# Feed-forward inputs with the activations held in TensorE and the weights passing, and a way through DRAM that turns the results

## The chip, the cores and the metric

The kernel runs on one core of one Trainium2 chip. The metric is the device time of one execution in microseconds (us), taken as the median of several runs. Of the core's engines, TensorE (PE) multiplies, VectorE (DVE), ScalarE (ACT) and GpSimd (POOL) do the work element by element, and SyncE (SP) issues most of the transfers.

## The reference

A small decoder trunk: 256 positions of width 1024, two layers, float32. Each layer is a feed-forward half step, a mixer (a gated short convolution in the first layer, sparse attention in the second), and another feed-forward half step. So there are four feed-forwards, which this change is about:

```
def rmsnorm(x, g):
    xf = x.astype(jnp.float32)
    y = xf * lax.rsqrt(jnp.mean(xf * xf, axis=-1, keepdims=True) + EPS)
    return (y * g.astype(jnp.float32)).astype(x.dtype)

def swiglu_ffn(x, w_in, w_out):          # w_in: 1024 x 5632, w_out: 2816 x 1024
    gate, up = jnp.split(x @ w_in, 2, axis=-1)
    return (jax.nn.silu(gate) * up) @ w_out

for i in range(DEPTH):
    ...
    h = h + 0.5 * swiglu_ffn(rmsnorm(h, ffn1_norm[i]), ffn1_w_in[i], ffn1_w_out[i])
    hn = rmsnorm(h, mix_norm[i])
    h = h + (short_conv_mixer(hn, ...) if i < N_A_LAYERS else nsa_mixer(hn, ..., kv))
    h = h + 0.5 * swiglu_ffn(rmsnorm(h, ffn2_norm[i]), ffn2_w_in[i], ffn2_w_out[i])
```

## The kernel before

The residual h lies in SBUF turned, with features on partitions: 8 tiles of 128 features x 256 positions. Every number that goes into a product is split in two (hi and lo, both in TensorE's fp32r form), and three of the four partial products are made: hi x hi, lo x hi, hi x lo. A tile of activations, xs[k], is 128 x 512: 256 positions of hi, then 256 of lo.

Weights come as one long stream (class Stream). A load brings 128 x 2048 numbers (1 MB) into one of three ws buffers; ScalarE casts half of such a load to hi (high, tile wh), VectorE subtracts to get lo (low, tile wl). Such a half is a unit of 128 x 1024; up to six units are held. take hands units to the products, done gives them back, and pump splits as many further ones as there is room for. Where pump, high and low are called in the program sets the order in which ScalarE and VectorE do this work between their other work. All engines run their own instructions in the order of the program and wait for each other by semaphores.

A feed-forward's input (ffn_in) makes 22 hidden tiles of 128 features. For each tile f it holds the weights in TensorE and lets the activations pass: for gate and for up, 8 wide matmuls (wh[k] held, xs[k] with all 512 columns passing, which gives hi x hi and lo x hi side by side) and 8 narrow ones (wl[k] held, the 256 hi columns passing). From the fifth tile on, two tiles are interleaved (lines 425 and 430). The result is in PSUM with hidden features on partitions: total adds the two halves (L367, L368), times multiplies by the norm's factor per position (R, 128 x 256; L372), ffn_evac applies Silu and multiplies (L384, L385), and split makes the hi and lo of the hidden tile hid[f] (L361, L362). The factor R comes from Norm.rows: a matmul of all ones with the sums of squares gives it on all partitions.

The projection out (out_proj) holds a tile of w_out and lets hid[f] pass, 22 wide and 22 narrow matmuls for each of 8 output tiles (L498, L504), mostly two output tiles interleaved. out_evac adds the result to h and makes the next stage's xs.

The first feed-forward is different at its start: first_tiles makes three hidden tiles while the inputs still arrive (L574), and their sums wait for the norm's factor.

The K/V projection (b_full, L762 to L764) and the queries' projection already hold activations: per k and per half of the positions (tt), hi is held and wh passes (512 columns), lo is held and wh passes, hi is held and wl passes. The result has positions on partitions.

Of the kernel before, what the change touches and what calls it, by code (L numbers as in the profile page):

```python
# [12 lines left out]
AF = mybir.ActivationFunctionType  # L13
# [3 lines left out]
P = 128  # L17
# [24 lines left out]
THIRD = {1: (0, 2), 3: (2, 4), 6: (4, 8)}  # L42
LINE, FIXED = 256, 160
HOMES = (("ones", [P, P], F32), ("V0", [P, 512], F32), ("V1", [P, 512], F32), ("vc", [P, 2, 2, 64], F32R),
         ("cs0", [P, 8, 4, 16], F32R), ("cs1", [P, 8, 4, 16], F32R), ("cbias", [P, 8, 2, 2, 16], F32),
# [23 lines left out]
def trunk(ctx, tc, A, out):  # L69
# [29 lines left out]
    def bank2():  # L99
        return mk([P, 2, 512], "mm", 2, pool=ps)  # L100
# [300 lines left out]

    def ffn_in(xs, norm, R=None, bg=None, pre=None, sums=()):

        hid, sums = [], list(sums)
        box = [R]
        n0 = len(sums)

        def mid():
            if pre is not None:
                pre()  # L410
            box[0] = norm.rows()

        def finish(f, o):
            sums.append(total(o, 2))
            late = len(sums) > 1
            weave(ffn_evac(sums.pop(0), box[0], hid), not late or f == n0 + 5)
            if late and f - n0 in (3, 7, 9):
                list(ffn_evac(sums.pop(0), box[0], hid))
            if bg is not None:
                bg(f)  # L420

        def wide(o, us, ks, last=8):
            for x in range(2):
                for k in ks:
                    pe.matmul(o[:, x], us[x][0][:, k * P:(k + 1) * P], xs[k], start=(k == 0), stop=(k == last))  # L425

        def narrow(o, us, last=8):
            for x in range(2):
                for k in range(8):
                    pe.matmul(o[:, x, :T], us[x][1][:, k * P:(k + 1) * P], xs[k][:, :T], start=False, stop=(k == last))  # L430

        f = n0
        while f < NF:
            o = bank2()
            if f < n0 + 4 or f + 1 == NF:
                a_group([o[:, 0], o[:, 1]], xs, mid if f == n0 and R is None else None, not n0)
                finish(f, o)
                f += 1
                continue

            u = W.take(2)
            wide(o, u, range(8))
            o2, u2 = bank2(), W.take(2)
            wide(o2, u2, [0])
            narrow(o, u, 7)
            W.done(2, False)
            finish(f, o)
            narrow(o2, u2)
            wide(o2, u2, range(1, 8), 7)
            W.done(2, False)  # L450
            finish(f + 1, o2)
            f += 2
        return hid

# [17 lines left out]

    def out_proj(lhs, factor, norm, final=False):

        n, i, u = len(lhs), 0, None
        head = []
        if n == 8:
# [29 lines left out]

        c = len(head)
        while c < ND - final:
            o, run = bank(), []  # L510
            if n > 8 and c % 2 and c + 1 < ND - final:
                wide(o, run, range(n))
                o2, run2 = bank(), []
                wide(o2, run2, [0])
                narrow(o, run, range(n), n - 1)
                out_evac(o, c, factor, norm)
                narrow(o2, run2, range(n), free=False)
                wide(o2, run2, range(1, n), n - 1)
                for _ in range(sum(t[2] for t in run2)):
                    W.done(1, False)  # L520
                out_evac(o2, c + 1, factor, norm)
                W.pump()
                c += 2
                continue
            for ks in (range(n - 1), [n - 1]) if c == 0 else (range(n),):
                wide(o, run, ks)
                narrow(o, run, ks, n - 1)
            out_evac(o, c, factor, norm, n == 8)
            c += 1
# [135 lines left out]

    sums, parts_sq = first_tiles()
    hid = ffn_in(xs, First(), sums=sums)
    xs = new_xs()
    nm = Norm([(xs, G_MIX)])
    out_proj(hid, 0.5, nm)  # L670
    nm.halves()
# [67 lines left out]

    hid = ffn_in(xs, nm, pre=lambda: list(tab), bg=bias_bg)  # L740

# [4 lines left out]
    nm = Norm([(xkv, G_KV), (xs, G_FFN1 + 8)])  # L746
    out_proj(hid, 0.5, nm)
    nm.halves()
# [61 lines left out]
    def kv_cols(k):  # L810
# [4 lines left out]
        for tt in range(2):  # L815
            pe.transpose(pt[:, tt * P:(tt + 1) * P], kv["R"][:, tt * P:(tt + 1) * P], ident)
        kv["rc"] = sm([P, 2])
        ve.tensor_copy(out=kv["rc"], in_=pt[:, 0:2 * P:P])
# [165 lines left out]

    hid = ffn_in(xs, None, R1, bg)
    xs = new_xs()
    nm = Norm([(xs, G_MIX + 8)])
    out_proj(hid, 0.5, nm)
    del hid
# [333 lines left out]
    del oT  # L1323
    hid = ffn_in(xs, nm)

# [3 lines left out]

    out_proj(hid, 0.5, Store(), True)  # L1330

# [8 lines left out]
def _layout(i):  # L1340
# [3 lines left out]
    for n in ("ffn1", "ffn2"):  # L1344
        w = a[n + "_w_in"]
        r[n + "_w_in"] = w.reshape(2, 8, 128, 2, NF, 128).transpose(0, 2, 4, 3, 1, 5).reshape(2, 128, -1)
        r[n + "_w_out"] = np.stack([_rows(w) for w in a[n + "_w_out"]])

# [62 lines left out]
```

## Time and profile before

| | |
|---|---|
| median of 3 runs | 964.38 us (964.18 to 964.45) |
| the profiled execution | 964.34 us, span 962.6 us |
| TensorE matmuls | busy 958.2 us (100% of the span), 5618 recorded |
| VectorE, ScalarE, GpSimd | busy 725.5, 580.7, 128.8 us |
| traffic | 178.14 MB, 185 GB/s in the mean |
| TensorE's granted clock | 0.999 |

A matmul's duration in the trace runs from its issue to its modelled end and overlaps the next one's, so the distance from start to start says what one costs. Rows of a timeline give the start, the time, the engine, the line, and how many instructions were merged; rows of groups give the busy time, the mean duration of one in ns, and the idle time before them with what ended it.

### The profile page before, as it was taken

The page shows a single profiled execution, that of the slowest core. Times are in us where ns is not written, and L with a number is a line of the kernel's source. Part 1 is how long each engine was busy: PE and PEld are TensorE (multiplying, and loading weights), DVE is VectorE, ACT ScalarE, POOL GpSimd, SP SyncE. Part 2 cuts the span into 40 slices and gives each one's busy share as a digit, 9 for nine tenths or more (in the row PEclk, how much of TensorE's full clock was granted, in tenths as well). Part 3 has the DMA queues.
Part 4 walks back from the last instruction along what each step waited for, and adds up shares of the span by engine and source line. Part 5 has one row for each costly group of instructions (what it writes and reads, how often), then busy time and mean ns, then how long its engine had stood idle before and what let it go on. Part 6 is the DMA issues. An engine that isn't in the chain of part 4 may idle for free.

```text
span 962.6 us, 14572 instructions
## 1 busy us (share of the span) xinstructions
PE 958.2 (100%) x5618; PEld 841.9 (87%) x5618; DVE 725.5 (75%) x1154; ACT 580.7 (60%) x984; POOL 128.8 (13%) x212
## 2 busy tenths in 40 slices
PE   9999999999999999999999999999999999999998
PEld 8888888888888888888888888889877888888888
DVE  7898875678898787765758789767589798778643
ACT  7666653555466665644648876745489776566430
POOL 2000001154420000000121012000147110000000
PEclk9999999999999999999999999999999999999999
DMA  8565544545546874545536566445511256455541
GB/s 308 219 219 189 205 175 175 209 176 195 188 173 221 233 236 176 196 158 215 219 132 203 189 216 246 175 175 210 193 44 46 92 211 224 175 192 202 180 158 57
DMA packets 28898, 178.14 MB, mean 185 GB/s; under 512 B 3179, under 2 KB 6763, under 8 KB 8220
## 3 DMA queue, kind: packets, MB, share of 16 engines
q1 hardware_dynamic: 28684, 176.95, 51.1%
q8 instruction: 44, 0.72, 0.3%
q10 hardware_dynamic: 144, 0.26, 0.1%
q14 instruction: 26, 0.21, 0.1%
HBM read 175.59 MB, written 1.08 MB: 184 GB/s over the span
## 4 chain that ended last, share of the span: by engine, by line
PE 99%; ACT 0%; DVE 0%; issue 0%
PE mm L425 26%; PE a L498 17%; PE mm L430 14%; PE mm L353 10%; PE a L504 9%; PE mm L358 5%; PE a L353 4%; PE a L358 2%; PE mm L1127 1%; PE mm L574 1%; PE a L1204 1%; PE a L762 1%; PE a L764 1%; PE a L763 1%; PE a L1172 1%; PE a L574 1%
## 5 line engine op out<-in xcount | busy, mean ns | idle before, releaser
L182 DVE TENSOR_TENSOR wl<-ws,wh 128x1024 fp32r<-128x1024 f32 x318 | 392.5, 1251 | 48.1 <-ACT wh L165 30.9
L165 ACT CAST wh<-ws 128x1024 fp32r<-128x1024 f32 x318 | 327.0, 1045 | 35.8 <-PE a L498 12.3
L425 PE MATMUL mm<-xs,wh 128*128 128x512 f32 x1088 | 254.9, 390 | 0.0
L425 PEld LDWEIGHTS mm<-xs,wh 128*128 128x128 f32 x1088 | 201.6, 188 | 40.1
L498 PE MATMUL a<-act,wh 128*128 128x512 f32 x714 | 167.0, 390 | 0.0
L498 PEld LDWEIGHTS a<-act,wh 128*128 128x128 f32 x714 | 132.7, 188 | 26.8
L430 PEld LDWEIGHTS mm<-xs,wl 128*128 128x128 f32 x1088 | 135.3, 192 | 2.6
L430 PE MATMUL mm<-xs,wl 128*128 128x256 f32 x1088 | 136.8, 283 | 0.0
L368 DVE TENSOR_TENSOR t<-mm,t 128x512 f32<-128x512 f32 x95 | 65.4, 688 | 72.9 <-ACT t L367 72.2
L367 ACT COPY t<-mm 128x512 f32<-128x512 f32 x95 | 55.6, 586 | 94.2 <-PE mm L430 47.0
L353 PE MATMUL mm<-xs,wh 128*128 128x512 f32 x400 | 96.8, 392 | 0.0
L504 PEld LDWEIGHTS a<-act,wl 128*128 128x128 f32 x714 | 89.0, 192 | 1.8
L504 PE MATMUL a<-act,wl 128*128 128x256 f32 x714 | 89.9, 283 | 0.0
L353 PEld LDWEIGHTS mm<-xs,wh 128*128 128x128 f32 x400 | 73.3, 188 | 13.9
L314 POOL TENSOR_TENSOR sq<-sq,t 128x256 f32<-128x256 f32 x35 | 27.7, 791 | 389.1 <-ACT t L312 389.0
L457 DVE SCALAR_TENSOR_TENSOR base<-a,base 128x256 f32<-128x256 f32 x78 | 32.8, 422 | 57.0 <-PE a L498 54.7
L297 ACT ACTIVATE xs<-base 128x256 fp32r<-128x256 f32 x48 | 24.0, 504 | 79.0 <-DVE base L457 69.7
L384 ACT ACTIVATE t<-t 128x256 f32<-128x256 f32 x88 | 36.8, 418 | 52.7 <-DVE t L372 52.7
L372 DVE TENSOR_TENSOR t<-t,R 128x512 f32<-128x512 f32 x88 | 61.5, 699 | 2.6
L361 ACT CAST act<-t 128x256 fp32r<-128x256 f32 x96 | 39.0, 407 | 29.8 <-DVE t L691 19.4
L358 PEld LDWEIGHTS mm<-xs,wl 128*128 128x128 f32 x400 | 52.1, 191 | 2.4
L358 PE MATMUL mm<-xs,wl 128*128 128x256 f32 x400 | 52.8, 283 | 0.0
(274 smaller groups left out, 910.7 us busy)
## 6 DMA issues: line engine op xcount, KB each, us to landing
ws<-in_ffn_w_in_dram SPq DMA_DIRECT2D x85, 1024.0 KB, 4.7
ws<-in_ffn_w_out_dram SPq DMA_DIRECT2D x44, 1024.0 KB, 4.6
ws<-in_conv_w_in_dram SPq DMA_DIRECT2D x12, 1024.0 KB, 4.6
ws<-in_w_kv_dram SPq DMA_DIRECT2D x6, 1024.0 KB, 5.3
ws<-in_conv_w_out_dram SPq DMA_DIRECT2D x4, 1024.0 KB, 4.8
ws<-in_attn_w_q_dram SPq DMA_DIRECT2D x4, 1024.0 KB, 4.9
ws<-in_attn_w_o_dram SPq DMA_DIRECT2D x4, 1024.0 KB, 4.9
base<-row_d SPq DMA_DIRECT2D x8, 256.0 KB, 6.1
```

The lines of the kernel that those rows point to most:

```text
L165: ac.copy(h, src)
L182: ve.tensor_tensor(out=l, in0=src, in1=h.bitcast(F32), op=ALU.subtract)
L353: pe.matmul(o, u[0][:, k * P:(k + 1) * P], xs[k], start=(k == 0), stop=False)
L358: pe.matmul(o[:, :T], u[1][:, k * P:(k + 1) * P], xs[k][:, :T], start=False, stop=(k == last))
L361: ac.copy(dst[:, :T], src)
L367: ac.copy(r, o[:, :, T:])
L368: ve.tensor_tensor(out=r, in0=o[:, :, :T], in1=r, op=ALU.add)
L372: ve.tensor_tensor(out=r, in0=r, in1=R[:, None, :].to_broadcast([P, n, T]), op=ALU.mult)
L425: pe.matmul(o[:, x], us[x][0][:, k * P:(k + 1) * P], xs[k], start=(k == 0), stop=(k == last))
L430: pe.matmul(o[:, x, :T], us[x][1][:, k * P:(k + 1) * P], xs[k][:, :T], start=False, stop=(k == last))
L498: pe.matmul(o, run[k][0], lhs[k], start=(k == 0), stop=(k == last))
L504: pe.matmul(o[:, :T], run[k][1], lhs[k][:, :T], start=False, stop=(k == last))
```

## The change

All four feed-forward inputs are now made like the K/V projection (ffn_tokens). A pair g of hidden tiles (256 hidden features) is one pass: the weights are laid out so that 512 columns hold 256 gate and 256 up features, and per k and per half of the positions three matmuls of 512 columns are made. The first feed-forward keeps the old form for its first four tiles (a shortened ffn_in) and does so from pair 2 on.

The result has positions on partitions and features along the row, and out_proj needs it the other way round. So per pair: ScalarE applies Silu to the gate half straight from PSUM, with the norm's factor as its scale per partition; VectorE multiplies by the up half and by the factor, and turns blocks of 32 x 32 in place (turned). The tile of 128 x 2 x 256 is written to DRAM (sent), and read back in another order of its blocks, 32 numbers at a time (placed). That leaves features on partitions in an order of its own, which the rows of w_out follow (a new layout on the host). Then the tile is split into hi and lo as before (halved). These steps are spread over the next pairs: pair g is turned and sent at k = 1 of pair g + 1, read back at k = 7 of it (k = 5 if it is the last pair, then on ScalarE's queue instead of SP's), and split at k = 5 of pair g + 2. The last pair is sent and read back on ScalarE's queue after the loop, and split by rest(), which out_proj calls after the first 20 of 22 hidden tiles of its first two output tiles. The factor per position comes from Norm.cols, per partition, and is taken at the last k of a stage's first pair; the third feed-forward uses the factors of the K/V stage (rc).

```diff
+FROM = {"ffn1": (2, 0), "ffn2": (0, 0)}
...
+    def ffn_in(xs, norm, sums):
+
+        hid, sums, box = [], list(sums), []
+        us = W.take(2)
+        o = bank2()
+        a_pass([(o[:, x], us[x], xs, range(8)) for x in range(2)], mid=lambda: box.append(norm.rows()))
+        W.done(2, False)
+        sums.append(total(o, 2))
+        for r in sums:
+            weave(ffn_evac(r, box[0], hid))
+        return hid
+
+    def ffn_tokens(xs, norm=None, rc=None, bg=None, pre=None, hid=()):
+
+        hid, box = list(hid), [rc]
+        n0, last = len(hid) // 2, NF // 2 - 1
...
+        def turned(o):
+            rc, tb = box[0], t2([P, 2, T])
+            for tt in range(2):
+                s = t1()
+                ac.activation(s, o[:, tt, :T], AF.Silu, scale=rc[:, tt:tt + 1])
+                ve.scalar_tensor_tensor(out=s, in0=o[:, tt, T:], scalar=rc[:, tt:tt + 1], in1=s, op0=ALU.mult, op1=ALU.mult)
+                ve.transpose(tb[:, tt], s)
+            return tb
+
+        def sent(tb, eng):
+            d = mk([2, P, T], "turn", 3, pool=dr)
+            eng.dma_start(d.rearrange("t p n -> p t n"), tb)
+            return d
+
+        def placed(d, eng):
+            ht = t2([P, 2, T])
+            eng.dma_start(ht.rearrange("p f (c j) -> p f c j", j=32), d.rearrange("t (a i) (c f j) -> (i c) f (t a) j", i=32, f=2, j=32))
+            return ht
...
+        for g in range(n0, last + 1):
+            o = bank2()
+            for k in range(8):
+                if k % 2 == 0:
+                    u, = W.take()
+                if k == 7 and box[0] is None:
+                    mid()
+                wh, wl = [u[x][:, (k % 2) * 512:(k % 2 + 1) * 512] for x in range(2)]
+                for tt in range(2):
+                    sh, sl = xs[k][:, tt * P:(tt + 1) * P], xs[k][:, T + tt * P:T + (tt + 1) * P]
+                    pe.matmul(o[:, tt], sh, wh, start=(k == 0), stop=False)
+                    pe.matmul(o[:, tt], sl, wh, start=False, stop=False)
+                    pe.matmul(o[:, tt], sh, wl, start=False, stop=(k == 7))
+                if k % 2 == 0:
+                    continue
+                if k == 1 and old is not None:
+                    way = sent(turned(old), sy)
+                if k == 5 and ready is not None:
+                    halved(ready)
+                    ready = None
+                if k == (5 if g == last else 7) and way is not None:
+                    ready, way = placed(way, ac if g == last else sy), None
+                W.done(1, g < last or k < 7)
+            old = o
...
+        tb = turned(old)
+        halved(ready)
+        ready = placed(sent(tb, ac), ac)
+        W.pump()
+        return hid, lambda: halved(ready)
...
+        if rest is not None:
+            runs = [(bank(), []) for _ in range(2)]
+            for x, (o, run) in enumerate(runs):
+                run += [tile() for _ in range(n)]
+                wide(o, run, range(n - 2))
+                narrow(o, run, range(n - 2), n - 1, not x)
+            rest()
+            for x, (o, run) in enumerate(runs):
+                wide(o, run, range(n - 2, n))
+                narrow(o, run, range(n - 2, n), n - 1, False)
...
-    hid = ffn_in(xs, First(), sums=sums)
+    hid = ffn_in(xs, First(), sums)
+    hid, rest = ffn_tokens(xs, nm, hid=hid)
...
-    out_proj(hid, 0.5, nm)
+    out_proj(hid, 0.5, nm, rest=rest)
```

How it moves instructions. On TensorE, in the middle of a feed-forward, before: a tile's held weights change with every matmul and the activations pass (mm is the PSUM tile, and the operand behind the arrow is the passing one first).

```order
L425 MATMUL mm_566<-xs_121,wh_497 128x512
L425 MATMUL mm_566<-xs_122,wh_497 128x512
L425 MATMUL mm_583<-xs_115,wh_543 128x512
L425 MATMUL mm_583<-xs_115,wh_550 128x512
L430 MATMUL mm_566<-xs_115,wl_492 128x256
L430 MATMUL mm_566<-xs_116,wl_492 128x256
```

The same place after:

```order
L461 MATMUL mm_1029<-wh_981,xs_122 128x512
L462 MATMUL mm_1029<-wh_981,xs_122 128x512
L463 MATMUL mm_1029<-wl_985,xs_122 128x512
L461 MATMUL mm_1117<-wh_1005,xs_115 128x512
L462 MATMUL mm_1117<-wh_1005,xs_115 128x512
L463 MATMUL mm_1117<-wl_1007,xs_115 128x512
```

All matmuls are 512 wide now, and one pair follows the other without interleaving.

On VectorE, at the start of the first feed-forward, before (wl are weights' lo parts, act hidden tiles, the t tiles their way from PSUM):

```order
L362 TENSOR_TENSOR act_397<-t_58_388,act_397 128x256
L368 TENSOR_TENSOR t_64_433<-mm_400,t_64_433 128x512
L372 TENSOR_TENSOR t_39_295<-t_39_295,R_362 128x512
L182 TENSOR_TENSOR wl_439<-ws_336,wh_437 128x1024
L385 TENSOR_TENSOR t_67_441<-t_67_441,t_39_295 128x256
L182 TENSOR_TENSOR wl_448<-ws_336,wh_444 128x1024
L362 TENSOR_TENSOR act_450<-t_67_441,act_450 128x256
L368 TENSOR_TENSOR t_73_486<-mm_453,t_73_486 128x512
L372 TENSOR_TENSOR t_41_316<-t_41_316,R_362 128x512
L182 TENSOR_TENSOR wl_492<-ws_393,wh_490 128x1024
```

And after:

```order
L363 TENSOR_TENSOR act_397<-t_58_388,act_397 128x256
L183 TENSOR_TENSOR wl_402<-ws_336,wh_400 128x1024
L183 TENSOR_TENSOR wl_408<-ws_336,wh_404 128x1024
L373 TENSOR_TENSOR t_39_295<-t_39_295,R_362 128x512
L386 TENSOR_TENSOR t_68_411<-t_68_411,t_39_295 128x256
L363 TENSOR_TENSOR act_414<-t_68_411,act_414 128x256
L373 TENSOR_TENSOR t_41_316<-t_41_316,R_362 128x512
L386 TENSOR_TENSOR t_70_418<-t_70_418,t_41_316 128x256
L363 TENSOR_TENSOR act_421<-t_70_418,act_421 128x256
L373 TENSOR_TENSOR t_55_380<-t_55_380,R_362 128x512
L386 TENSOR_TENSOR t_72_425<-t_72_425,t_55_380 128x256
L363 TENSOR_TENSOR act_428<-t_72_425,act_428 128x256
```

The three waiting hidden tiles are finished one after the other with no weights between them; before, one tile's steps alternated with weights.

On ScalarE, at the end of the first feed-forward, before (the last two tiles leave PSUM between casts of weights):

```order
L367 COPY t_219_1312<-mm_1243 128x512
L165 CAST wh_1316<-ws_1219 128x1024
L384 ACTIVATE t_222_1320<-t_219_1312 128x256
L165 CAST wh_1323<-ws_1219 128x1024
L361 CAST act_1329<-t_222_1320 128x256
```

After, from the read of the next-to-last pair to the split of the last (turn is the tile in DRAM):

```order
L441 DMA t_224_1181<-turn_1139 128x16x32
L166 CAST wh_1183<-ws_1113 128x1024
L429 ACTIVATE t_228_1200<-mm_1117,rc_493 128x256
L429 ACTIVATE t_229_1204<-mm_1117,rc_493 128x256
L362 CAST act_1208<-t_224_1181 128x256
L362 CAST act_1211<-t_224_1181 128x256
L436 DMA turn_1214<-t_227_1199 128x2x256
L441 DMA t_233_1216<-turn_1214 128x16x32
L166 CAST wh_1218<-ws_1113 128x1024
L166 CAST wh_1263<-ws_1159 128x1024
L166 CAST wh_1275<-ws_1159 128x1024
L362 CAST act_1325<-t_233_1216 128x256
```

ScalarE issues the last transfers itself, and waits in its own row for what they need. On SP, in the same stage, before there were weight loads alone:

```order
L138 DMA ws_1063<-in_ffn_w_in_dram 128x2048
L138 DMA ws_1113<-in_ffn_w_in_dram 128x2048
L138 DMA ws_1169<-in_ffn_w_out_dram 128x2048
L138 DMA ws_1219<-in_ffn_w_out_dram 128x2048
L138 DMA ws_1275<-in_ffn_w_out_dram 128x2048
```

After, up to the end of the stage:

```order
L436 DMA turn_1051<-t_195_1042 128x2x256
L139 DMA ws_1071<-in_ffn_w_out_dram 128x2048
L441 DMA t_208_1109<-turn_1051 128x16x32
L139 DMA ws_1113<-in_ffn_w_out_dram 128x2048
L436 DMA turn_1139<-t_213_1130 128x2x256
L139 DMA ws_1159<-in_ffn_w_out_dram 128x2048
L139 DMA ws_1220<-in_ffn_w_out_dram 128x2048
```

Per pair a write and a read stand between the two loads.

More of the change, by code (lines that the diff above doesn't have):

```diff
@@ L400, in a_group @@
         W.done(len(parts), False)
[L402 to L406, printed above, removed]
+    def ffn_in(xs, norm, sums):
[11 more added lines that the diff above has]
+        n0, last = len(hid) // 2, NF // 2 - 1
         def mid():
@@ L410, in mid @@
                 pre()
[L411 to L418, printed above, removed]
-            if bg is not None:
[L420 to L452, printed above, removed]
@@ L453, in ffn_in @@
-        return hid
+            box[0] = norm.cols()
+        def turned(o):
[10 more added lines that the diff above has]
+            return d
@@ new lines, in placed, with halved @@
+        def placed(d, eng):
+            ht = t2([P, 2, T])
+            eng.dma_start(ht.rearrange("p f (c j) -> p f c j", j=32), d.rearrange("t (a i) (c f j) -> (i c) f (t a) j", i=32, f=2, j=32))
+            return ht
+        def halved(ht):
+            for f in range(2):
+                hd = act()
+                split(ht[:, f], hd)
+                hid.append(hd)
+        ready, old, way = None, None, None
+        for g in range(n0, last + 1):
[22 more added lines that the diff above has]
+            old = o
+            if bg is not None:
+                bg(2 * g)
+                bg(2 * g + 1)
@@ L471, in out_evac, with out_proj @@
             norm.low(c)
-    def out_proj(lhs, factor, norm, final=False):
+    def out_proj(lhs, factor, norm, final=False, rest=None):
         n, i, u = len(lhs), 0, None
+        if rest is not None:
+            n = NF
         head = []
@@ L508, in out_proj @@
         c = len(head)
+        if rest is not None:
+            runs = [(bank(), []) for _ in range(2)]
[7 more added lines that the diff above has]
+                narrow(o, run, range(n - 2, n), n - 1, False)
+            for _ in range(sum(t[2] for t in runs[1][1])):
+                W.done(1, False)
+            for x, (o, run) in enumerate(runs):
+                out_evac(o, x, factor, norm)
+            W.pump()
+            c = 2
         while c < ND - final:
@@ L738, in bias_bg @@
             c_bias(f - 13)
-    hid = ffn_in(xs, nm, pre=lambda: list(tab), bg=bias_bg)
+    hid, rest = ffn_tokens(xs, nm, bg=bias_bg, pre=lambda: list(tab))
     xs = new_xs()
@@ L746, in trunk @@
     nm = Norm([(xkv, G_KV), (xs, G_FFN1 + 8)])
-    out_proj(hid, 0.5, nm)
+    out_proj(hid, 0.5, nm, rest=rest)
     nm.halves()
@@ L816, in kv_cols @@
             pe.transpose(pt[:, tt * P:(tt + 1) * P], kv["R"][:, tt * P:(tt + 1) * P], ident)
-        kv["rc"] = sm([P, 2])
+        kv["rc"] = mk([P, 2], "rc", 2)
         ve.tensor_copy(out=kv["rc"], in_=pt[:, 0:2 * P:P])
@@ L983, in bg @@
             c_values(kv["av"])
-    hid = ffn_in(xs, None, R1, bg)
+    hid, rest = ffn_tokens(xs, rc=rc, bg=bg)
     xs = new_xs()
     nm = Norm([(xs, G_MIX + 8)])
-    out_proj(hid, 0.5, nm)
+    out_proj(hid, 0.5, nm, rest=rest)
     del hid
@@ L1323, in trunk @@
     del oT
-    hid = ffn_in(xs, nm)
+    hid, rest = ffn_tokens(xs, nm)
     class Store:
@@ L1328, in tile @@
             sy.dma_start(out[c][:, q], h[c][:, q])
-    out_proj(hid, 0.5, Store(), True)
+    out_proj(hid, 0.5, Store(), True, rest)
 def _rows(w):
@@ L1345, in _layout @@
         w = a[n + "_w_in"]
-        r[n + "_w_in"] = w.reshape(2, 8, 128, 2, NF, 128).transpose(0, 2, 4, 3, 1, 5).reshape(2, 128, -1)
-        r[n + "_w_out"] = np.stack([_rows(w) for w in a[n + "_w_out"]])
+        ins, outs = [], []
+        for w, v, g in zip(w.reshape(2, 1024, -1), a[n + "_w_out"], FROM[n]):
+            one = w.reshape(8, 128, 2, NF, 128).transpose(1, 3, 2, 0, 4).reshape(128, NF, -1)[:, :2 * g]
+            two = w.reshape(8, 128, 2, NF // 2, 256).transpose(1, 3, 0, 2, 4).reshape(128, NF // 2, -1)[:, g:]
+            ins.append(np.concatenate([one.reshape(128, -1), two.reshape(128, -1)], 1))
+            turned = v[256 * g:].reshape(-1, 4, 2, 32, 1024).transpose(0, 2, 3, 1, 4).reshape(-1, 1024)
+            outs.append(_rows(np.concatenate([v[:256 * g], turned])))
+        r[n + "_w_in"], r[n + "_w_out"] = np.stack(ins), np.stack(outs)
     third = r["ffn1_w_in"][0][:, 4096:6144].reshape(128, 2, 8, 128).transpose(0, 2, 1, 3).reshape(128, -1)
```

## The prediction

> **What bounds the kernel now.** First the page's busy times and its chain that ended last.
>
> ```profile
> PE 958.2 (100%) x5618; PEld 841.9 (87%) x5618; DVE 725.5 (75%) x1154; ACT 580.7 (60%) x984; POOL 128.8 (13%) x212
> ...
> PE 99%; ACT 0%; DVE 0%; issue 0%
> ```
>
> TensorE is on the chain for 99% of the span, so the time is the sum of its matmuls' distances from start to start. Their durations (390 and 283 ns) overlap and must not be added. So I read those distances in the timeline of TensorE, first in the second feed-forward, where one row is one run of equal matmuls:
>
> ```profile
> 305.63 4.00 PE L430 MATMUL mm<-xs,wl 128*128 128x256 f32 x32
> 309.47 7.44 PE L425 MATMUL mm<-xs,wh 128*128 128x512 f32 x32
> 316.75 4.00 PE L430 MATMUL mm<-xs,wl 128*128 128x256 f32 x32
> ...
> 394.54 4.00 PE L430 MATMUL mm<-xs,wl 128*128 128x256 f32 x32
> ```
>
> Two hidden tiles (32 wide, 32 narrow matmuls) take (394.54 - 305.63) / 8 = 11.114 us, of which the narrow ones 309.47 - 305.63 = 3.84 us, 120 ns each, and the wide ones 7.28 us, 227 ns each. A narrow one has half the columns and costs 53%: 227 - 120 = 107 ns for 256 columns leaves 13 ns that come with every matmul, whatever its width. The form that the change brings (activations held, 512 weights passing) is in this kernel already, in the K/V projection (b_full):
>
> ```profile
> 468.85 0.39 PE L762 MATMUL a<-wh,t 128*128 128x512 f32 x1
> 469.07 0.39 PE L763 MATMUL a<-wh,t 128*128 128x512 f32 x1
> 469.30 0.39 PE L764 MATMUL a<-wl,t 128*128 128x512 f32 x1
> ...
> 471.57 0.39 PE L762 MATMUL a<-wh,t 128*128 128x512 f32 x1
> ```
>
> Twelve of these take 471.57 - 468.85 = 2.72 us, 227 ns each: the same pace as a wide one.
>
> **The change, part by part.** *Matmuls.* A pair of hidden tiles goes from 32 x 227 + 32 x 120 ns to 48 x 227 = 10.90 us; the columns are the same, 16 matmuls fewer carry the 13 ns. That saves 0.214 us per pair. The first feed-forward has 9 such pairs and the others 11 each, 42 in all: -9.0 us, all of it on the path. The weight loads (48 of 188 ns per pair, 9.0 us) stay below the matmuls.
>
> [...]
>
> *Norm.* Where the other layout needs the factor per column (cols), four one-column matmuls replace two of 256. The queries' projection shows what four such cost:
>
> ```profile
> 695.78 0.50 PE L1005 MATMUL a<-ones,sq 128*128 128x1 f32 x4
> 696.14 0.49 PE L762 MATMUL mm<-wh,xs 128*128 128x512 f32 x1
> 696.47 0.40 PE L763 MATMUL mm<-wh,xs 128*128 128x512 f32 x1
> ```
>
> 0.36 us, and 0.33 - 0.23 us on the next matmul: 0.46 us. In the second and fourth feed-forward the old form goes for about as much, the third gets its factors from the K/V stage, the first now computes both: +0.46 us once, at most +1.4 if the old form were free.
>
> *Vector and scalar work.* The groups by shape:
>
> ```profile
> L182 DVE TENSOR_TENSOR wl<-ws,wh 128x1024 fp32r<-128x1024 f32 x318 | 392.5, 1251 | 48.1 <-ACT wh L165 30.9 <-PE a L504 14.7 <-issue 2.2
> L368 DVE TENSOR_TENSOR t<-mm,t 128x512 f32<-128x512 f32 x95 | 65.4, 688 | 72.9 <-ACT t L367 72.2
> L372 DVE TENSOR_TENSOR t<-t,R 128x512 f32<-128x512 f32 x88 | 61.5, 699 | 2.6
> L362 DVE TENSOR_TENSOR act<-t,act 128x256 fp32r<-128x256 f32 x96 | 40.5, 421 | 5.2 <-ACT act L361 5.2
> L361 ACT CAST act<-t 128x256 fp32r<-128x256 f32 x96 | 39.0, 407 | 29.8 <-DVE t L691 19.4 <-DVE t L385 2.8
> L385 DVE TENSOR_TENSOR t<-t,t 128x256 f32<-128x256 f32 x88 | 37.4, 425 | 3.6 <-ACT t L384 3.5
> L384 ACT ACTIVATE t<-t 128x256 f32<-128x256 f32 x88 | 36.8, 418 | 52.7 <-DVE t L372 52.7
> L457 DVE SCALAR_TENSOR_TENSOR base<-a,base 128x256 f32<-128x256 f32 x78 | 32.8, 422 | 57.0 <-PE a L498 54.7 <-PE a L358 0.7 <-PE a L504 0.2
> L333 DVE RECIPROCAL R<-t 128x256 f32<-128x256 f32 x4 | 7.0, 1746 | 3.7 <-ACT t L331 3.7
> ```
>
> Per pair VectorE does 4 x 1.25 + 2 x (0.69 + 0.70 + 0.43 + 0.42) = 9.5 us now. After, it does 5.0 + 2 x (0.42 + transpose + 0.42). No row shows a block transpose: it lies between 0.42 (the other operations of its shape) and 1.75 us (the reciprocal of that shape). I take 0.45, since it also reads and writes each element once: 7.6 us, and even at the upper bound 10.2 of 10.9. ScalarE loses its copy out of PSUM. Nothing here is on the path, but the order of these steps is, at two places.
>
> *Start of the first feed-forward.* The order shows that the products of tiles 2, 3 and 4 are now finished one behind the other, three instructions each, ahead of the next weights. VectorE and ScalarE wait for each other in each: 0.69 + 0.46 + 0.45 + 0.45 + 0.38 = 2.45 us. In the timeline:
>
> ```profile
> 27.85 3.82 PE L353 MATMUL mm<-xs,wh 128*128 128x512 f32 x16
> 29.61 1.28 ACT L384 ACT_TABLE_LOAD   x1
> 33.43 0.42 DVE L362 TENSOR_TENSOR act<-t,act 128x256 fp32r<-128x256 f32 x1
> ```
>
> Up to 33.85 us both kernels run alike. Then two weight splits (to 36.25) and three times 2.45 (to 43.6); the next wl is there at 45.45. TensorE wants it in the second half of its second pair, two of the 227 ns behind that half's start: 27.85 + 10.90 + 0.46 + 5.45 + 0.45 = 45.1. It waits 0.35 us. ScalarE then goes through two splits, a table load of 1.28 for the root, one more split, a table load for Silu, and the first pair leaves PSUM at 51.85; the third pair, which needs those banks, is due at 50.45: 1.4 us. Together +1.75 us; 0 if the pairs of engines overlap better than I think, 4 if the transpose is at its upper bound.
>
> *The way through DRAM.* Per pair one write of 256 KB and one read of 256 KB in 2,048 pieces of 128 bytes. No transfer here has such pieces; the traffic nearest in size, first 256 pieces of 512 bytes (960.2 to 961.4 us), then 48 of 64 bytes or less (204.8 to 205.1 us):
>
> ```profile
> q1 hardware_dynamic: 288, 0.13, 37.6%
> ...
> q1 hardware_dynamic: 48, 0.00, 8.3%
> ```
>
> 0.376 x 16 x 1.2 us / 256 = 28 ns, and 0.083 x 16 x 0.3 / 48 = 8 ns. So a read keeps each of the 16 engines busy for 128 x (8 to 28 ns) = 1.1 to 3.6 us. The traffic of the second feed-forward as it is (the last columns are TensorE's clock, the DMA share and GB/s):
>
> ```profile
> 301.75:390.24 88.49, 88.49 (x512) 78.38 (x511) 70.33 (x98) 52.81 (x80) 3.06 (x16) 1.00 0.67 214
> ```
>
> 0.67 x 88.49 us for 214 GB/s x 88.49 us = 18.9 MB is 3.1 us per MB. A pair needs 2 MB, 6.3 us, plus 0.8 for the write and 1.1 to 3.6 for the read: 8.2 to 10.7 of 10.9 us. It fits, near 9 if the price is proportional to size. SP now waits twice per pair, for the transposes (4.1 us into a pair) and for the write's landing, with a weight load behind each. Three buffers of ws give a load some 9 us from there; it takes 4.7:
>
> ```profile
> ws<-in_ffn_w_in_dram SPq DMA_DIRECT2D x85, 1024.0 KB, 4.7
> ...
> base<-row_d SPq DMA_DIRECT2D x8, 256.0 KB, 6.1
> ...
> out_dram<-base SPq DMA_DIRECT2D x7, 128.0 KB, 1.7
> ```
>
> So inside a stage nothing reaches TensorE. POOL gets no new work; the background steps of the second and third feed-forward (bg) now come two at a time at a pair's end instead of one per tile, in the same order and at the same distance from their users, and cost nothing as long as POOL, busy for 3.06 of 88 us in the row above, follows.
>
> *End of each stage.* Count from the start of the last pair (it ends at 10.9). The next-to-last pair is transposed by 4.1, written and, on ScalarE's queue, read back, cast and split (0.83); the projection out wants it in its 19th matmul, at 10.9 + 18 x 0.227 = 15.0. The last pair is transposed by 13.3, takes the same two legs, and is wanted after 40 steps of the projection:
>
> ```profile
> 931.10 10.00 PE a L498 x44
> 941.10 5.27 PE a L504 x44
> ```
>
> (10.00 + 5.27) / 44 = 0.347 us a step, so at 10.9 + 13.9 = 24.8. Both come in time as long as a leg takes up to 4.7 us from issue to landing. The write stands ahead of the load in SP's order, with empty rings before it: 2 to 2.5 us, as the stores above (1.7 us for half as much). The read has ScalarE's ring to itself: 2.7 to 4.5 us (that of the store, plus 1.1 to 3.6, less the store's own). Its issue keeps ScalarE itself:
>
> ```profile
> 312.53 0.34 SPq L138 DMA_DIRECT2D ws<-in_ffn_w_in_dram  x1
> 312.92 0.43 SPq L725 DMA_DIRECT2D base<-row_d  x1
> ```
>
> 128 pieces take 0.34 us to issue, 256 take 0.43; by that 2,048 could take up to 1.7. ScalarE also stands still until the last write has landed (about 15.8), with three weight casts behind it; the first of these is wanted at 21.9, so 2 us more do no harm. I take no wait at these ends; up to 1 us a stage is possible.
>
> **Sum.** -9.0 + 0.46 + 1.75 = -6.8 us. The profiled execution took 964.34 us (span 962.6 and 1.7 around it), 0.04 below the median: 957.5 us.
>
> **Rivals.** *A, legs not covered.* The 6.1 us of the row_d transfers, each behind a weight load, speak for long legs. With legs of L us the next-to-last pair is cast by 4.1 + 2L + 0.82; only then does ScalarE send the last pair, which is ready at 5.75 + 4L instead of 24.8: 4L - 19.05 us late (L above 4.75). At 6.1 that is 5.4 us, four times, and 964.3 - 6.8 + 21.4 = 979 us. Slower than before by 0.2% from L = 5.3 on. Against it: the order puts nothing ahead of the two transfers there. [...] Chance 0.14.
>
> *B, no fixed part.* If the new matmuls ran at the average pace of the old pair's columns (11.114 / 48 = 232 ns), nothing would be saved and the 0.46 + 1.75 us remain: 966.5 us, at the edge of 0.2%. Against it stand the twelve matmuls of b_full. Chance 0.06. [...]
>
> *C, small waits at several turns.* 1 to 2 us at each stage's end, or 4 at the first start: 962.5 to 964.5 us. For it: the next-to-last pair's way has under 2 us to spare at legs of 4. Chance 0.08.
>
> **How the numbers follow.** The forecast, with waits between 0 and 4 us in place of 1.75, has 0.72 and reaches from 955.3 (all 9.0 kept) to 962; the range goes on through C, to 964.5. What is left out is A, B and a little below. A measurement here tells 0.2%, 1.9 us, from no change. Faster: 0.72 and the better third of C, 0.75; same: the rest of C and B, 0.11; slower: A, 0.14.
>
> **What would show it.** The profile after should have 42 x 16 = 672 fewer matmuls (about 4,950), pairs of 10.9 us without gaps, VectorE's share falling by about 80 us, a gap of one to two us near 50 us, and none at the projections out. A TensorE that waits for act tiles behind a DMA would show A; matmuls 232 ns apart, B.

## The result, and the profile after

| | time, us | ratio to before, 95% interval |
|---|---|---|
| before | 964.56 (964.18 to 965.17, 6 runs) | 1 |
| after | 972.31 (971.18 to 974.62, 6 runs) | 1.0082 [1.0069, 1.0095] |

The change made the kernel 0.8% slower, 7.75 us; 957.5 us, 0.7% faster, had been forecast, and the range ended at 964.5. The profiled execution after took 972.12 us with a span of 970.3 (before: 964.34 and 962.6), so the trace has 7.7 us to explain. Its page, busy times and the chain that ended last:

```profile
PE 955.0 (98%) x4954; PEld 809.8 (83%) x4954; DVE 660.4 (68%) x1071; ACT 536.3 (55%) x901; POOL 131.5 (14%) x212
...
PE 83%; DMA 7%; ACT 5%; DVE 2%; issue 1%; POOL 1%; SPq 0%; ACTq 0%; DVEq 0%
```

TensorE is no longer 99% of the chain but 83%: transfers and ScalarE now end waits. First the expected gain, in a window over eight pairs of the second feed-forward (the columns after the busy time are the clock, the DMA share and GB/s):

```profile
310.00:397.00 87.00, 87.00 (x385) 1.00 0.92 268
```

TensorE is busy all through. 87.0 us hold eight pairs of 48 matmuls, 226.7 ns each: 10.88 us a pair where it was 11.114. Over 42 pairs that is -9.8 us. The gain is there, and something of 17 us stands against it. The timeline of TensorE shows where it waits (the bracket is the idle time ahead of the row, and what ended it):

```profile
52.29 0.47 PE L461 MATMUL mm<-wh,xs 128*128 128x512 f32 x1 [1.29 <-DVE t L430]
...
133.50 0.84 PE L529 MATMUL a<-act,wh 128*128 128x512 f32 x2 [0.68 <-DVE act L363]
...
405.81 0.83 PE L529 MATMUL a<-act,wh 128*128 128x512 f32 x2 [0.85 <-DVE act L363]
...
565.60 0.59 PE L929 MATMUL a<-wh,act 128*128 128x256 f32 x3 [1.36 <-DVE wh L178]
...
636.87 1.22 PE L529 MATMUL a<-act,wh 128*128 128x512 f32 x2 [6.16 <-DVE act L363]
```

L529 is the projection out, at its 19th matmul, where it takes up the hidden tiles of the next-to-last pair. It waits in three of four feed-forwards, longest in the third. L461 is the start of the first feed-forward, L929 a background step with weights of its own (joint). By their distances from start to start these five cost 1.45, 0.84, 1.0, 1.5 and 6.3 us. The releaser is VectorE's split (L363), but VectorE had itself been idle for 3.9 us before it: the tiles came late. ScalarE's timeline ahead of that gap shows why:

```profile
615.77 2.00 ACT L166 CAST wh<-ws 128x1024 fp32r<-128x1024 f32 x2 [1.83 <-DMA ws<-in_ffn_w_out_dram]
617.79 1.28 ACT L970 ACT_TABLE_LOAD   x1
619.09 0.32 ACT L970 ACTIVATE t<-a,epst 128x64 f32<-128x64 f32 x1
...
621.43 1.28 ACT L429 ACT_TABLE_LOAD   x1
622.73 0.47 ACT L429 ACTIVATE t<-mm,rc 128x256 f32<-128x256 f32 x1
...
627.61 0.61 ACTq L441 DMA_DIRECT2D t<-turn  x1
...
635.96 0.40 ACT L362 CAST act<-t 128x256 fp32r<-128x256 f32 x1 [4.41 <-DMA t<-turn]
```

The pair's last matmul ends at 615.0, and the last pair's first one starts at 615.45. The finished pair's Silu (L429) stands in ScalarE's row behind two background steps (L970 and what follows) with a table load before and after, and behind a wait for a weight load; it starts at 622.73. So the read is issued at 627.61, 12.2 us into the last pair instead of 6.7. And the read is slow. The view of the turned tiles' transfers, for this one:

```profile
L441 ACTq DMA_DIRECT2D t<-turn x1: 606/606/606, 627.6 to 627.6; - x1
DMA to landing us min/median/max: 8.3/8.3/8.3
```

8.3 us, where 2.7 to 4.5 had been assumed; it took 8.2 and 8.3 in the first and second feed-forward, and 7.1 in the fourth, which didn't wait. What moved meanwhile is in the view of the DMA queues for these 8.3 us (queue, packets, MB, share of the 16 engines; q1 is SP's, q10 ScalarE's):

```profile
q1 hardware_dynamic: 270, 1.95, 62.8%
q10 hardware_dynamic: 2064, 0.26, 20.1%
```

So beside the 0.26 MB of the read 1.95 MB of weights moved, two loads' worth, and their packets took three times the read's share of the 16 engines (1.94 MB and 60.4%, the read 21.0%, in the first feed-forward). Before the change the same background steps stood in ScalarE's row too, but 12.8 us ahead of the projection out, where it was 8.6 after:

```profile
612.33 1.28 ACT L922 ACT_TABLE_LOAD   x1
...
616.60 1.28 ACT L384 ACT_TABLE_LOAD   x1 [1.24 <-DVE t L372]
```

The projection out began at 625.11 there, and TensorE didn't wait for it. Then comes a cost that stands in no wait. The window behind the gap:

```profile
635.20:642.00 6.80, 5.13 (x22) 4.98 (x23) 2.93 (x4) 3.66 (x5) 0.00 (x0) 0.50 0.37 80
```

For 6.8 us the granted clock is 0.50, and TensorE is busy for 5.13 of them. The 20 narrow matmuls there take 4.2 us where the next 20 take 2.4; with the two wide ones ahead of them that is 2.4 us lost.

### The profile page after: what moved, and what is told of

It is laid out like the page before. It is cut to its first block, busy times and chain, and to the rows that moved or that the text cites. A ratio compares the mean times of both kernels' runs of the same rounds, so it can differ in the third digit from the quotient of the medians.

```text
span 970.3 us, 13458 instructions
## 1 busy us (share of the span) xinstructions
PE 955.0 (98%) x4954; PEld 809.8 (83%) x4954; DVE 660.4 (68%) x1071; ACT 536.3 (55%) x901; POOL 131.5 (14%) x212
## 4 chain that ended last, share of the span: by engine, by line
PE 83%; DMA 7%; ACT 5%; DVE 2%; issue 1%; POOL 1%; SPq 0%; ACTq 0%; DVEq 0%
PE a L529 16%; PE mm L461 11%; PE mm L462 11%; PE mm L463 11%; PE a L535 9%; PE mm L354 4%; PE a L354 4%; DMA t<-turn 3%; DMA ws<-in_ffn_w_in_dram 2%; PE mm L359 2%; PE a L359 2%; ACT wh L166 2%; PE mm L1175 1%; PE mm L621 1%; DMA ws<-in_ffn_w_out_dram 1%
## 5 line engine op out<-in xcount | busy, mean ns | idle before, releaser
L461 PE MATMUL mm<-wh,xs 128*128 128x512 f32 x672 | 262.5, 391 | 1.3 <-DVE t L430 1.3
L463 PE MATMUL mm<-wl,xs 128*128 128x512 f32 x672 | 262.0, 390 | 0.2
L462 PE MATMUL mm<-wh,xs 128*128 128x512 f32 x672 | 261.5, 389 | 0.0
L529 PE MATMUL a<-act,wh 128*128 128x512 f32 x714 | 170.0, 392 | 7.7 <-DVE act L363 7.7
L529 PEld LDWEIGHTS a<-act,wh 128*128 128x128 f32 x714 | 132.2, 188 | 35.0 <-DVE act L363 9.1
L463 PEld LDWEIGHTS mm<-wl,xs 128*128 128x128 f32 x672 | 126.1, 188 | 28.0 <-DVE wl L183 1.6
L461 PEld LDWEIGHTS mm<-wh,xs 128*128 128x128 f32 x672 | 126.2, 188 | 27.2 <-issue 1.7
L462 PEld LDWEIGHTS mm<-wh,xs 128*128 128x128 f32 x672 | 126.2, 188 | 25.9
L429 ACT ACTIVATE t<-mm,rc 128x256 f32<-128x256 f32 x84 | 39.7, 473 | 52.0 <-DVE t L430 46.3
L430 DVE SCALAR_TENSOR_TENSOR t<-mm,rc,t 128x256 f32<-128x256 f32 x84 | 40.5, 482 | 22.2 <-ACT t L429 19.1
L363 DVE TENSOR_TENSOR act<-t,act 128x256 fp32r<-128x256 f32 x96 | 36.8, 420 | 13.2 <-ACT act L362 13.2
L431 DVE STREAM_TRANSPOSE t<-t 128x256 f32<-128x256 f32 x84 | 37.4, 445 | 2.9
L354 PE MATMUL mm<-xs,wh 128*128 128x512 f32 x144 | 34.7, 391 | 0.0
L302 DVE SCALAR_TENSOR_TENSOR xs<-base,xs 128x256 fp32r<-128x256 f32 x48 | 27.9, 585 | 8.3 <-ACT xs L298 8.3
```

The source lines that it names most:

```text
L354: pe.matmul(o, u[0][:, k * P:(k + 1) * P], xs[k], start=(k == 0), stop=False)
L429: ac.activation(s, o[:, tt, :T], AF.Silu, scale=rc[:, tt:tt + 1])
L430: ve.scalar_tensor_tensor(out=s, in0=o[:, tt, T:], scalar=rc[:, tt:tt + 1], in1=s, op0=ALU.mult, op1=ALU.mult)
L431: ve.transpose(tb[:, tt], s)
L461: pe.matmul(o[:, tt], sh, wh, start=(k == 0), stop=False)
L462: pe.matmul(o[:, tt], sl, wh, start=False, stop=False)
```

## The experiments

Two theories were set against each other. The first: ScalarE's row (the background steps ahead of the Silu) makes the end of the third feed-forward late. The second: the leg of the read alone does. To these come the start and SP's queue as terms of their own. All times were taken beside runs of the kernel before (964.4 to 964.5 in each of the three groups); "less than after" compares them with the 972.31 us above, beside which it ran at 964.56. Rows and gaps are those of one execution of each kernel, and where its time lies far from the median the text says so.

**The background steps later.** In the last pair, three steps on instead of at the end of the pair before:

```
+                if k == 3 and g == last and bg is not None:
+                    bg(2 * g - 2)
+                    bg(2 * g - 1)
...
-            if bg is not None:
+            if bg is not None and g != last - 1:
```

> The background steps of the second and third feed-forward that came at the end of the next-to-last pair's turn come three steps later, behind the sending of that pair's tiles. Theory 1 (ScalarE's row: the two steps and their table loads stand ahead of the Silu of the next-to-last pair, which is sent 6 us late): the 6.3 us gap of the third feed-forward falls to about the 0.8 to 1.0 us of the first and second, the 6.8 us at half clock behind it go too (3.4 us), together -8 to -9 us, about 963.5 us, and in the trace the Silu of that pair starts within 2 us of its matmuls' end. Theory 2 (the transfers alone are late, 8.3 us of a read): the gap stays at 5 us or more and the time within 1 us of 972.

963.96 us (962.65 to 966.8), ratio 1.000 [0.9991, 1.0009]: 8.3 us less than after, as the first theory had it. ScalarE's timeline and the read's leg:

```profile
616.22 0.46 ACT L429 ACTIVATE t<-mm,rc 128x256 f32<-128x256 f32 x1
...
622.98 0.62 ACTq L441 DMA_DIRECT2D t<-turn  x1
```

```profile
L441 ACTq DMA_DIRECT2D t<-turn x1: 617/617/617, 623.0 to 623.0; - x1
DMA to landing us min/median/max: 3.7/3.7/3.7
```

The Silu is 6.5 us earlier (2.2 us behind its pair's last matmul instead of 7.7), the gap 0.57 us, and no half clock follows. But the leg shrank too, from 8.3 to 3.7 us, without having been touched: sent 4.6 us earlier, the read meets only the end of one load and the start of the next, 0.67 MB instead of 1.95. So the run doesn't part the theories as cleanly as meant.

**The read on SP.**

```
-                    ready, way = placed(way, ac if g == last else sy), None
+                    ready, way = placed(way, sy), None
```

> The read of each next-to-last pair is issued by SP, behind one weight load, in place of ScalarE. Theory 1 (on ScalarE's queue the read shares the 16 DMA engines with two weight loads at once, 8.2 us; behind one load on the same ring it takes some 5): the gaps of 0.84 and 1.0 us in the first and second feed-forward go, that of the third shrinks from 6.3 to about 3, and a pause of 3 us may leave the clock alone: -4 to -8 us, 964 to 968 us. Theory 2 (2,048 pieces of 128 bytes take 8 us whatever stands beside them): gaps and time unchanged, 972 us.

965.13 us (962.46 to 966.34; the profiled one 963.26), ratio 1.0002 [0.9994, 1.0011]: 7.2 us less than after. The Silu of the third feed-forward is late still (619.78), and yet the gap falls from 6.3 to 1.7 us; those of the first two are gone. The legs of the first and the third:

```profile
L441 SPq DMA_DIRECT2D t<-turn x1: 597/597/597, 124.2 to 124.2; - x1
DMA to landing us min/median/max: 5.5/5.5/5.5
```

```profile
L441 SPq DMA_DIRECT2D t<-turn x1: 591/591/591, 624.6 to 624.6; - x1
DMA to landing us min/median/max: 4.7/4.7/4.7
```

The late Silu with a shorter leg leaves 1.7 us, so most of the gap needed both causes together.

**The read right behind the write**, ahead of the weight load that stood between (at k == 3, the result kept until the pair's end):

```
-                if k == (5 if g == last else 7) and way is not None:
-                    ready, way = placed(way, ac if g == last else sy), None
+                if k == (3 if g == last else 7) and way is not None:
+                    nxt, way = placed(way, sy), None
...
+            ready, nxt = nxt, None
```

> The read of each next-to-last pair stands on SP's queue directly behind that pair's write, ahead of the weight load that came between. Theory 1 (the leg is 8.3 us only because loads share the DMA engines; alone it is some 3.3): the waits of 0.84 and 1.0 us go, that of the third feed-forward is 6.3 - 5 = 1.3 us or less, no half clock: 963 to 965 us, no worse than with the read one load later (965.1). Theory 2 (SP, waiting for the write, holds back the projection's first weights): a new wait for weights of 1 to 3 us at each end, 966 us or more.

964.77 us (963.1 to 967.47; the profiled one 963.1), ratio 1.0007 [0.9998, 1.0016], as with the read one load later. The leg of the first stage is 4.6 us, not 3.3, with 0.52 MB of loads beside it; that of the third is 3.3, with 0.13 MB. The held-back loads cost too, as the second theory feared, though only at the third projection out: 1.2 us for a weight, 0.9 us for the last tiles. And a pause of 1.82 us for the joint weights (at 560.67) was followed by a half clock of 3.4 us here:

```profile
560.00:562.00 2.00, 0.95 (x9) 0.75 (x7) 1.87 (x5) 1.58 (x4) 1.48 (x3) 1.00 0.00 0
562.00:564.00 2.00, 1.39 (x9) 1.35 (x10) 2.00 (x3) 2.00 (x4) 0.00 (x0) 0.96 0.82 197
564.00:566.00 2.00, 2.00 (x6) 1.47 (x6) 2.00 (x4) 0.43 (x1) 0.00 (x0) 0.50 0.81 291
```

**Without the way through DRAM**: `sent` and `placed` hand on the transposed tile itself.

> Leaves out the way through DRAM: the transposed tile is cast and split as it is, so hidden tiles lie in their blocks' old places; all matmuls, transposes and splits stay. Theory 1 (end waits of stages come from the read's leg and, in the third, from ScalarE's row): no gap at the first and second projection out, and the third keeps what ScalarE's row alone causes, the Silu 6 us late less the two legs of 10.5 us that fall away, that is no gap: with the half clock gone too, -11 to -12 us, 960 to 961 us, which leaves 1.45 us at the start and the background waits. Theory 2 (the row alone would still be late): third gap of 2 us or more, about 966 us.

957.56 us (957.22 to 958.13), ratio 0.993 [0.9918, 0.9943]. No wait is left at any projection out, and the background waits of the third feed-forward are gone as well; of the gaps above only that of the start stays (1.43 us). Both theories had this too slow (960 to 961, and 966). The number is the forecast's own, 957.5: what it left out, 14.75 us, comes with the way through DRAM as a whole. (That the two agree to 0.1 us is partly luck, since the matmuls saved 0.8 us more than forecast.) What had not been seen is the joint weights at 565.60. SP's timeline of the kernel after:

```profile
540.91 0.59 SPq L441 DMA_DIRECT2D t<-turn  x1
551.71 0.38 SPq L436 DMA_DIRECT2D turn<-t  x1
552.18 0.42 SPq L139 DMA_DIRECT2D ws<-in_cmp_w_k_dram  x1
```

and without the way:

```profile
537.34 0.33 SPq L139 DMA_DIRECT2D ws<-in_cmp_w_k_dram  x1
```

With the change the load stands on SP behind a write that waits for the next pair's transposes; without it, it is issued 15 us earlier.

**The tiles' traffic on ScalarE's queue**, for the pairs before the next-to-last, and the write two steps later:

```
-                    way = sent(turned(old), sy)
+                    tb = turned(old)
+                if k == (1 if g == last else 3) and old is not None:
+                    way = sent(tb, sy if g == last else ac)
...
-                    ready, way = placed(way, ac if g == last else sy), None
+                    ready, way = placed(way, ac), None
```

> Writes and reads of hidden pairs before the next-to-last go through ScalarE's queue, the write two steps later than the transposes, so that SP carries weight loads alone until the last pair; the ends of the stages are left as they are. Theory 1 (SP's row, which waits for the transposes, holds the joint weights' load back from 537 to 552 us): the load is issued by 540, the waits of 1.5, 0.5 and 0.7 us in the third feed-forward go, -2 to -3 us against the kernel after, 969.5 to 970.5 us with the 6.3 us gap still there. Theory 2 (VectorE, with the turned tiles' steps ahead of the joint splits, is late by itself): the 1.5 us wait stays and the time is within 1 us of 972.

966.92 us (964.68 to 971.09), ratio 1.0029 [1.0016, 1.0042]: 5.4 us less than after, twice what was expected. The profiled execution took 968.98, 3.1 us less than that of after, so these rows don't show the whole of it. The load is issued at 541.98 and the waits of 1.5, 0.5 and 0.7 us are gone, as the first theory said; the third gap is 4.9 instead of 6.3. On the other hand the second feed-forward now waits 3.1 us (at 404.37). There ScalarE, about to issue the read of the pair before, waits for its write to land:

```profile
390.82 0.59 ACTq L441 DMA_DIRECT2D t<-turn  x1
391.51 1.05 ACT L166 CAST wh<-ws 128x1024 fp32r<-128x1024 f32 x1 [2.91 <-DMA turn<-t]
392.46 0.47 ACT L429 ACTIVATE t<-mm,rc 128x256 f32<-128x256 f32 x1
```

The next-to-last pair's Silu (390.82 in the kernel after) is 1.64 us later by that, its read 1.58 us, and the tiles come as much later. Here ScalarE, which also computes, paid for that wait of its DMA issue with its own row. After that pause of TensorE the clock stayed at 1.00 (402 to 418 us).

**The start, spread.** The three waiting tiles put one each between the next pair's steps:

```
-        for r in sums:
-            weave(ffn_evac(r, box[0], hid))
-        return hid
+        weave(ffn_evac(sums.pop(0), box[0], hid))
+        return hid, [ffn_evac(r, box[0], hid) for r in sums]
...
+                if late:
+                    list(late.pop(0))
```

> The finishing of tiles 2, 3 and 4 of the first feed-forward is spread over the first steps of the next pair, with weight splits between, instead of standing as one block ahead of them. Theory 1 (the block delays the splits, and with them the first turned pair's leaving PSUM): the gap of 1.45 us near 50 us goes, -1.5 us, about 970.8 us. Theory 2 (the gap comes from the table loads of root and Silu on ScalarE): the gap stays above 1 us, no change.

974.16 us (970.51 to 976.35), ratio 1.0095 [1.0078, 1.0113]. A miss for both: the gap grew to 3.2 us. Each tile still takes its 2.45 us of VectorE and ScalarE in turns, now with a split behind each, so the next one starts 4.2 us later instead of 2.4, and the block is longer. And with the pause of 3.2 us at 50.17 came a half clock:

```profile
52.80:59.60 6.80, 6.01 (x14) 4.77 (x15) 6.61 (x10) 4.75 (x7) 0.00 (x0) 0.50 0.73 211
```

**The start, in turns.** All three products, then all three Silu, then all three splits:

```
-        for r in sums:
-            weave(ffn_evac(r, box[0], hid))
+        gens = [ffn_evac(r, box[0], hid) for r in sums]
+        for _ in range(3):
+            for gen in gens:
+                next(gen, None)
+            W.pump(1)
+        W.pump()
```

> At the start of the first feed-forward the three waiting tiles are finished in turns (all three products with the factor, then all three Silu, then all three splits) in place of one after the other; nothing else moves. Theory 1 (VectorE and ScalarE wait for each other within each tile, 7.35 us for 4.6 us of VectorE's work, and all that follows on ScalarE is late by that): the block takes some 4.6 to 5 us, the gap of 1.45 us near 50 us goes, -1.5 us against the kernel after, about 970.8. Theory 2 (the two table loads and the casts of ScalarE's row set the gap): it stays above 1 us.

969.88 us (968.78 to 971.67), ratio 1.0058 [1.0046, 1.0071]: 2.4 us less than after. The first turned pair leaves PSUM 4.1 us earlier; this row starts at 50.12 in the kernel after:

```profile
46.00 0.47 ACT L433 ACTIVATE t<-mm,rc 128x256 f32<-128x256 f32 x1
```

The gap near 50 us is gone. (Some 0.9 us of the 2.4 are a third gap of 5.4 instead of 6.3 us; why that moved stays open.)

**All four together**: background steps later, read on SP, the other traffic on ScalarE's queue, the start in turns.

> All of it together: background steps of the next-to-last turn behind that pair's sending, the read of the next-to-last pair on SP, the turned tiles' other traffic on ScalarE's queue, the start's three tiles in turns. If the causes are the ones named and add up, nothing of the DRAM way is left on the path: the 957.6 us of the kernel without that way less the 1.45 us of the start, 956.1, up to 957.5 with small waits; no gap of over 0.6 us outside the attention. If they hide each other's successors, 960 us or more.

956.88 us (956.0 to 958.63), ratio 0.9924 [0.991, 0.9937]: faster than before by 0.8%. The changed kernel's waits are gone; the longest that is new is 0.5 us (at 354.19). Its page, and the window in which the joint weights had been late:

```profile
PE 950.5 (100%) x4954; PEld 807.7 (85%) x4954; DVE 660.8 (69%) x1071; ACT 537.3 (56%) x901; POOL 128.2 (13%) x212
...
PE 95%; DMA 3%; DVE 1%; ACT 1%; ACTq 0%; issue 0%
```

```profile
540.00:580.00 40.00, 40.00 (x187) 33.50 (x186) 28.08 (x42) 29.05 (x51) 8.59 (x14) 1.00 0.75 242
```

**One of the four left out at a time**, each against 956.88 us.

> As the kernel with all four edits (956.9 us), but the turned tiles' traffic before the last pair is back on SP's queue. If the edits' parts are separate, the wait of 1.5 to 1.9 us for the joint weights near 560 us comes back, with up to 1.5 us of half clock behind it: 958.5 to 960.5 us. If that wait was only a follower of the other ones: within 0.6 us of 956.9.

960.54 us (959.58 to 963.43): +3.7. The joint weights' pause of 1.9 us is back, the granted clock is 0.50 behind it (up to 1.7 us lost in 3.4), and the third projection out waits 0.84 us.

> As the kernel with all four edits (956.9 us), but the start's three tiles are finished one after the other again. The gap of 1.45 us near 50 us comes back: 958.3 us, no half clock. If the earlier 2.4 us that this edit alone brought are all its own: 959.3 us.

958.51 us (957.22 to 959.63): +1.6, the gap of 1.43 us at 50.19. The profiled execution took 959.53 and also waits 1.3 us at the second projection out (403.53). That isn't the part left out: ScalarE waits for a write to land ahead of the next-to-last pair's Silu, as in the kernel with the traffic on its queue.

> As the kernel with all four edits (956.9 us), but the background steps stand ahead of the next-to-last pair's Silu again. The Silu is late by 3 to 6 us; with the read on SP 1.7 us of that came through before: a gap of 1 to 2.5 us near 620 us, 958 to 960 us. If ScalarE's row costs by itself as much as the 6.3 us gap, without any help of the read's leg: 963 us or more.

957.15 us (956.47 to 958.01; the profiled one 958.01): +0.3, below what was expected. The Silu is late as foreseen (614.17; 609.78 in the next kernel, where the steps come later), but only 1.0 us of it reaches TensorE: with SP free of the other traffic, ScalarE doesn't wait for a weight load ahead of the steps (1.83 us in the kernel after), and the read's leg is 4.8 us, not 8.3. The second projection out waits 1.0 us here too, again behind a write on ScalarE's queue. That edit thus has a price of its own, which shows in some executions: 3.1, 1.3 and 1.0 us in three traces, nothing in that of all four edits.

> As the kernel with all four edits (956.9 us), but the next-to-last pair's read is issued by ScalarE again, beside two weight loads. Legs of 7 to 9 us: gaps of about 0.8, 1.0 to 3 and 0.6 us at the first three projections out, 959.3 to 961.3 us. If the leg does no harm once ScalarE's row is right: within 0.6 us of 956.9.

959.34 us (956.67 to 965.16, 11 runs): +2.5, with far more spread than any other kernel here. The profiled execution took 957.41 us, near the lowest, and its leg in the third feed-forward was 3.8 us; what the longer ones wait for isn't shown.

The four parts left out singly come to 3.7 + 1.6 + 0.3 + 2.5 = 8.1 us; put back together they are 15.4. The rest is some 7 us. The one gap that the late Silu and the slow leg made jointly, with its half clock, would be 6.3 + 2.4 us; that it is the rest is argued from the two runs that each heal it, not measured by itself.

## Why the prediction was wrong

*Matmuls, right.* Forecast 10.90 us a pair, measured 10.88; -9.0 against -9.8 us. 4,954 matmuls were named as about 4,950. Rival B is out: it allows no gain, and the kernel with all four edits is 7.5 us ahead of the kernel before, net of the factor.

*Work of VectorE and ScalarE, right in kind.* The block transpose was taken at 0.45 us:

```profile
51.15 0.45 DVE L431 STREAM_TRANSPOSE t<-t 128x256 f32<-128x256 f32 x1
```

VectorE's total fell by 65 us (80 named). Start of the first feed-forward: 1.4 us at 50.45 was forecast, 1.45 us at 50.61 measured; the earlier wait of 0.35 us didn't come. (The five terms of a tile add up to 2.43 us, not 2.45; 2.41 was measured.)

*"I take no wait at these ends": wrong, the first failed step.* The write's leg was right (2.3 us, 2 to 2.5 forecast). The read was sized by "ScalarE's ring to itself: 2.7 to 4.5 us". The ring was its own, the 16 engines were not: 8.2 to 8.3 us beside 1.9 MB of loads, 3.3 to 5.5 for the legs on SP's ring given above, and 3.4 us with nothing beside it (the last pair's read in the fourth feed-forward, 910.2 to 913.6). By the prediction's own count the tiles were due at S + 15.0; issued at S + 6.7 and 8.2 us under way, plus 0.83 to split them, they come at S + 15.7 (S is the last pair's start): 0.7 us late, and 0.84 was measured in the first feed-forward. The price of a piece was right (8 to 28 ns; about 13 measured, from the 20.1% of 8.3 us that 2,064 packets took on the 16 engines).

*"Cost nothing as long as POOL follows": wrong, the second failed step, and the dearest.* POOL followed, but for one wait of 0.7 us (at 591.41) that is gone once the joint weights come in time. The background steps cost through ScalarE: taken two at a time at a pair's end, they stand in its row ahead of the Silu of the pair just finished, with two table loads. So the Silu came 7.7 us behind its pair and the read was issued at S + 12.2; with the 8.3 us of the leg that made the gap of 6.3 us. The order printed ahead of the prediction showed ScalarE's row only in the first feed-forward, which has no background steps.

*"Inside a stage nothing reaches TensorE": wrong by 1.5 to 2.5 us.* The 9 us that three buffers give were worked out for plain weights. SP's wait for the transposes holds back the joint weights' load from 537 to 552 us, and 565.60 waits for it. Left out of the final version, that costs 3.7 us with its half clock.

*Half clock: no term of the sum.* A pause was priced at its length. The one of 6.3 us in the kernel after cost over a third as much again: 2.4 us behind it.

*Rival A* had the place (the legs at the stage ends) but not the mechanism: it charged 5.4 us four times with both legs at 6.1; measured were 0.84, 1.0, 6.3 and 0 us, all for the next-to-last pair and not the last. The sign named for it, TensorE waiting for act tiles behind a DMA, is what the profile shows. Its doubt was worth more than 0.14.

The items together: -9.8 (matmuls) + 0.5 (factor) + 1.4 (start) + 8.2 (gaps at three ends) + 2.4 (half clock) + 2.5 (background waits) = +5.2 us. Of the 7.7 some 2.5 remain. Half a microsecond of it lies in the program's start (the last matmul of L621 begins at 22.48, that of L574 before at 21.93); the rest was not tracked.

## What to carry over

When a hand-over that was local is put on a chain of several engines and queues, write down each engine's row between the hand-over's ends, in every stage and not in one, and ask what already stands there: here background work that had cost nothing stood in front of the one instruction that had become urgent. A transfer's leg is not its own bytes alone: the read of 0.26 MB took 3.4 us with nothing beside it, and 8.3 us beside 1.95 MB that the other queue had issued. Put waits for computed data on a queue that carries nothing urgent behind them (left out of the version with all four edits, that cost 3.7 us), and count a pause of TensorE with what it may cost in clock afterwards: here 2.4 us behind one of 6.3, and nothing behind one of 3.1.

## What was not expected of the hardware

The granted clock went to 0.50 with pauses of TensorE of 6.3 us (6.8 us long), 3.2 us (6.8 us) and 1.8 and 1.9 us (3.4 us each), but stayed at 1.00 through one of 3.1 us (second feed-forward, traffic on ScalarE's queue) and one of 1.9 us for the joint weights (the read on SP). So it isn't the pause's length alone that decides. Between 560 and 564 us, in the kernel with the read right behind the write, TensorE was idle for 1.66 us (the rows above), and the clock fell; between 560 and 566 us in the kernel with the read on SP it was idle for 1.98 us, and the clock stayed:

```profile
560.00:562.00 2.00, 1.76 (x10) 1.14 (x9) 0.47 (x1) 1.50 (x5) 1.71 (x3) 1.00 0.00 0
562.00:564.00 2.00, 0.50 (x4) 0.30 (x3) 1.86 (x5) 1.95 (x4) 1.09 (x2) 1.00 0.00 0
564.00:566.00 2.00, 1.76 (x11) 1.42 (x12) 2.00 (x4) 2.00 (x4) 0.00 (x0) 1.00 0.94 229
```

The times from one change of the clock to the next in the kernel after are 628.05, 6.83 and 327.68 us, which are 184, 2 and 96 times 3.413 us; in the kernel before the one recorded stretch at full clock is 955.73 us, 280 times that. What makes one pause end in a drop and another not isn't shown: no run moved a pause against the changes of the clock on purpose.
